# Rotary embedding on one core: two matmul rows of eight in place of three, VectorE sums the other six

## Chip, cores, metric

One core of a Trainium2 chip. The metric is the device time of the core in microseconds (us); the kernel before takes 163.04 us (median of 3 runs, 162.64 to 163.21). A profiled run also has a span, from its first to its last instruction, which here is about 2 us shorter than the device time (161.0 us for 163.02 us).

## The reference

```python
batch, seq, dim = (16, 512, 1024)        # fp32, 16 heads of 64
x = x.reshape(batch, seq, num_heads, head_dim)
x1, x2 = x[..., :half_dim], x[..., half_dim:]
rotated = np.concatenate([x1 * cos - x2 * sin, x1 * sin + x2 * cos], axis=-1)
```

The input is 32 MiB and so is the output; each element takes two products and a sum. cos and sin depend on the sequence position only.

## The kernel before

The data goes through in 8 tiles of 128 partitions x 8 rows x 1024 fp32, 4 MiB each, updated in place in 5 SBUF buffers (in the code NT is the 8 tiles, KK the 8 rows of a tile, P the 128 partitions). For each row two products are summed: `x*cos` (VectorE, into PSUM) and the half-swapped `x*sin`, called `b` (GpSimd, into SBUF). Two ways of summing exist:

- a TensorE row: VectorE writes `x*cos` as two 512-wide halves into single PSUM banks, an identity matmul adds `b` on top of each, ScalarE copies the result back to SBUF;
- a VectorE row: VectorE writes `x*cos` over a two-bank PSUM buffer (`pd`, two of them) and adds `b` itself.

Row 0 is special: VectorE forms its sin product too, in place, so that GpSimd has 7 rows of 8 to do.

```python
PE_ROWS = (0, 3, 6)
DVE_B = ((0,), (0,))
FIRST = (3, 8)
LAST_OUT = (4, 8)            # the last tile is stored in two halves
# ... pools: xp 5 tiles, bp 6 rows, PSUM: pe 3 banks, pd 2 x 2 banks, tables 1 bank
def add(most):
    while len(pending) > most:
        r, ps, b = pending.pop(0)
        nc.vector.tensor_tensor(out=r, in0=ps, in1=b, op=ALU.add)

def finish(t):
    add(0)
    lo = 0
    for hi in LAST_OUT if t == NT - 1 else (KK,):
        store(t, lo, hi)
        lo = hi
    if t + 1 == NT - BUFS:
        for n in range(BUFS, NT):
            load(n)
# ... loads of tiles 0 to 4 are issued at the start, all DMA from one queue (SyncE)
for t in range(NT):
    xt = tiles[t]
    for k in range(KK):
        r = xt[:, k * dim : (k + 1) * dim]
        own = k in DVE_B[t % 2]
        if not own:
            b = bp.tile([P, dim], FP32, name="b")
            # ...
            nc.gpsimd.tensor_tensor(out=halves(b), in0=swapped(r, nh), in1=over_heads(sk), op=ALU.mult)
        if k in PE_ROWS:
            # ... two 512-wide products into ps; for row 0 the sin product in place
            for ps, rc, rhs in parts:
                nc.tensor.matmul(out=ps, lhsT=ident, rhs=rhs, start=False, stop=True, skip_group_check=True)
                nc.scalar.copy(out=rc, in_=ps)
        else:
            add(1)
            ps = pd.tile([P, dim], FP32, name="pd")
            nc.vector.tensor_tensor(out=pairs(ps), in0=pairs(r), in1=cos_b(k, 2 * nh), op=ALU.mult)
            pending.append((r, ps, b))
        if k == 0 and t > 0:
            finish(t - 1)
        add(1)
finish(NT - 1)
```

## Time and profile before

| | before |
|---|---|
| device time, median | 163.04 us |
| span of the profiled run | 161.0 us |
| share of the DMA queue | 97.7% of 16 engines' span |
| VectorE / GpSimd busy | 131.6 / 130.2 us |
| end of VectorE | 142.3 us |
| last store issued, span ends | 142.81 us, 161.0 us |

The page of the kernel before: busy times, then its slices (each digit is the busy share of one of 40 slices, in tenths), then the DMA queue.

```profile
span 161.0 us, 614 instructions
...
PE 76.5 (48%) x103; PEld 24.5 (15%) x103; DVE 131.6 (82%) x142; ACT 29.4 (18%) x49; POOL 130.2 (81%) x62
...
DVE  1059998999999999999999999999999999930000
...
POOL 1039999999999999999999899999999999900000
...
DMA  5999999999999999999999999999999999999993
...
q1 hardware_dynamic: 2752, 67.24, 97.7%
```

VectorE (DVE) and GpSimd (POOL) go to zero in the last tenth of the span, the DMA engines go on.

The groups of VectorE and GpSimd before; after the bars: busy us, mean ns of one, idle time before them.

```profile
L164 POOL TENSOR_TENSOR b<-xt,sns 128x1024 f32<-128x1024 f32 x56 | 129.5, 2349 | 9.8 <-DVE sns L107 9.4
...
L144 DVE TENSOR_TENSOR xt<-pd,b 128x1024 f32<-128x1024 f32 x40 | 48.6, 1218 | 0.0
L182 DVE TENSOR_TENSOR pd<-xt,tab 128x1024 f32<-128x1024 f32 x40 | 48.2, 1223 | 0.3
...
L170 DVE TENSOR_TENSOR ps<-xt,tab 128x512 f32<-128x512 f32 x48 | 30.9, 688 | 0.6 <-ACT xt L178 0.6
```

VectorE in order of time, before (start, length, what). Starts, not lengths, give the cost, since consecutive instructions overlap.

```profile
17.98 1.22 DVE L182 TENSOR_TENSOR pd<-xt,tab 128x1024 f32<-128x1024 f32 x1
19.11 1.22 DVE L144 TENSOR_TENSOR xt<-pd,b 128x1024 f32<-128x1024 f32 x1
20.36 1.23 DVE L182 TENSOR_TENSOR pd<-xt,tab 128x1024 f32<-128x1024 f32 x1
...
139.91 2.35 DVE L144 TENSOR_TENSOR xt<-pd,b 128x1024 f32<-128x1024 f32 x2
```

From product to add there are 1.13 us, from that add to the next product 1.25 us: that product goes into the PSUM buffer which this very add sets free. The last line is where VectorE ends, at 142.26 us.

The SyncE queue before, its last DMA issue, and windows over the end (busy us and count of each engine, then clock, DMA share, GB/s). The columns are PE, PEld, DVE, ACT and POOL. A DMA packet (mostly 1.2 us long here) is counted whole in the window in which it starts, so a share can pass 1.00.

```profile
142.81 0.33 SPq L76 DMA_DIRECT2D out_dram<-xt  x1
```

```profile
138.00:142.00 4.00, 3.58 (x4) 1.17 (x4) 4.00 (x5) 0.59 (x1) 2.63 (x2) 0.50 1.06 459
142.00:150.00 8.00, 0.17 (x1) 0.00 (x0) 0.26 (x1) 0.58 (x1) 0.00 (x0) 0.50 0.94 406
150.00:156.00 6.00, 0.00 (x0) 0.00 (x0) 0.00 (x0) 0.00 (x0) 0.00 (x0) 0.50 1.01 434
```

VectorE ends at 142.26 us and ScalarE's last copy at 142.79 us. From then on no engine computes, and the DMA engines still run at full rate: they work off a backlog.

### The profile page before, as it was taken

To read this page: it belongs to the slowest core of one execution; us is meant where nothing else is said; L and a number is where in the kernel's file an instruction comes from. 1 tells how busy PE (TensorE), PEld (TensorE's weight loads), DVE (VectorE), ACT (ScalarE), POOL (GpSimd) and SP (SyncE) were. 2 spreads that over 40 slices of the span, in tenths; PEclk is the share of its full clock that TensorE was granted. 3 is DMA by queue.
4 is the path that set the end of the run, shared out by engine and by line. 5 is a ranking of instruction groups with operands and counts; after the bars stand their busy time and mean duration, and the time that the engine had idled before them with its cause. 6 is when DMAs were issued, how large, how long until landed. Compare 5 with 4: busy or idle time off the path is not lost.

```text
span 161.0 us, 614 instructions
## 1 busy us (share of the span) xinstructions
PE 76.5 (48%) x103; PEld 24.5 (15%) x103; DVE 131.6 (82%) x142; ACT 29.4 (18%) x49; POOL 130.2 (81%) x62
## 2 busy tenths in 40 slices
PE   3045808534766545618662751765266654630000
PEld 0022102110222012102210211121012210200000
DVE  1059998999999999999999999999999999930000
ACT  0110401402211221221122121212121122010000
POOL 1039999999999999999999899999999999900000
PEclk9999995987655697895579698678955579555555
DMA  5999999999999999999999999999999999999993
GB/s 174 407 412 472 391 488 423 391 464 448 391 440 474 391 415 488 399 415 480 407 415 472 407 415 466 423 415 448 423 423 448 431 423 431 448 415 415 427 436 155
DMA packets 2754, 67.26 MB, mean 418 GB/s; under 512 B 320, under 2 KB 448, under 8 KB 448
## 3 DMA queue, kind: packets, MB, share of 16 engines
q1 hardware_dynamic: 2752, 67.24, 97.7%
q14 instruction: 2, 0.02, 0.0%
HBM read 33.69 MB, written 33.55 MB: 418 GB/s over the span
## 4 chain that ended last, share of the span: by engine, by line
POOL 36%; DMA 22%; DVE 13%; issue 8%; PE 7%; POOLq 1%; ACT 1%; SPq 0%
POOL b L164 36%; DMA xt<-in_x_dram 18%; PE ps L177 6%; DVE xt L144 5%; DMA b<-in_sin_dram 4%; DVE pd L182 4%; DVE ps L170 3%; DVE xt L175 2%; POOLq L218 1%; PE tab L103 1%; ACT xt L178 1%; PE tab L104 1%; DVE sns L106 0%; SPq L72 0%; DVE sns L107 0%
## 5 line engine op out<-in xcount | busy, mean ns | idle before, releaser
L164 POOL TENSOR_TENSOR b<-xt,sns 128x1024 f32<-128x1024 f32 x56 | 129.5, 2349 | 9.8 <-DVE sns L107 9.4
L177 PE MATMUL ps<-b,ident 128*128 128x512 f32 x64 | 48.8, 906 | 43.3 <-POOL b L164 27.5
L144 DVE TENSOR_TENSOR xt<-pd,b 128x1024 f32<-128x1024 f32 x40 | 48.6, 1218 | 0.0
L182 DVE TENSOR_TENSOR pd<-xt,tab 128x1024 f32<-128x1024 f32 x40 | 48.2, 1223 | 0.3
L178 ACT COPY xt<-ps 128x512 f32<-128x512 f32 x48 | 28.1, 585 | 105.9 <-PE ps L177 105.9
L177 PE MATMUL ps<-xt,ident 128*128 128x512 f32 x32 | 24.2, 899 | 16.0 <-issue 6.6
L170 DVE TENSOR_TENSOR ps<-xt,tab 128x512 f32<-128x512 f32 x48 | 30.9, 688 | 0.6 <-ACT xt L178 0.6
L177 PEld LDWEIGHTS ps<-b,ident 128*128 128x128 f32 x64 | 15.2, 263 | 75.3 <-POOL b L164 56.6
L177 PEld LDWEIGHTS ps<-xt,ident 128*128 128x128 f32 x32 | 7.8, 268 | 33.2 <-issue 17.1
L175 DVE TENSOR_TENSOR xt<-xt,tab 128x1024 f32<-128x1024 f32 x8 | 9.8, 1221 | 0.4
L106 DVE TENSOR_SCALAR sns<-tab 128x256 f32<-128x256 f32 x1 | 0.4, 425 | 8.2 <-PE tab L104 8.2
L103 PE MATMUL tab<-b,spread 64*128 64x256 f32 x2 | 1.2, 694 | 5.1 <-DMA b<-in_sin_dram 5.1
L178 ACT ACT_TABLE_LOAD x1 | 1.3, 1283 | 7.5 <-DMA xt<-in_x_dram 7.5
L94 PE MATMUL ps<-zero 128*128 128x512 bf16 x3 | 1.5, 626 | 1.2 <-DVE zero L91 1.2
L103 PEld LDWEIGHTS tab<-b,spread 64*128 64x128 f32 x2 | 0.5, 310 | 6.0 <-issue 6.0
L104 PE MATMUL tab<-b,spread 64*128 64x256 f32 x2 | 1.1, 627 | 0.0
L91 DVE MEMSET zero<- 128x256 uint32 x1 | 0.3, 272 | 0.9 <-PEq L204 0.9
L104 PEld LDWEIGHTS tab<-b,spread 64*128 64x128 f32 x2 | 0.7, 329 | 0.2
L94 PEld LDWEIGHTS <-zero 128*128 128x128 bf16 x3 | 0.3, 125 | 1.5 <-DVE zero L91 1.2
L102 DVE COPY spread<-ident 64x64 f32<-64x64 f32 x2 | 0.3, 182 | 0.2 <-POOL ident masks.py:199 0.2
masks.py:197 POOL MEMSET ident<- 128x128 f32 x1 | 0.2, 204 | 0.3 <-POOLq L204 0.3
L107 DVE COPY sns<-tab 128x256 f32<-128x256 f32 x1 | 0.4, 415 | 0.0
(6 smaller groups left out, 0.9 us busy)
## 6 DMA issues: line engine op xcount, KB each, us to landing
xt<-in_x_dram SPq DMA_DIRECT2D x7, 4096.0 KB, 29.1
out_dram<-xt SPq DMA_DIRECT2D x7, 4096.0 KB, 28.4
out_dram<-xt SPq DMA_DIRECT2D x2, 2048.0 KB, 18.4
xt<-in_x_dram SPq DMA_DIRECT2D x1, 2560.0 KB, 11.5
xt<-in_x_dram SPq DMA_DIRECT2D x1, 1536.0 KB, 6.7
b<-in_sin_dram SPq DMA_DIRECT2D x1, 64.0 KB, 6.5
b<-in_cos_dram SPq DMA_DIRECT2D x1, 64.0 KB, 6.3
```

The lines of the kernel that those rows point to most:

```text
L94: nc.tensor.matmul(out=ps, lhsT=zero[:, :P], rhs=zero, start=True, stop=True)
L103: nc.tensor.matmul(out=sin_t, lhsT=spread, rhs=sin_sb, start=True, stop=True)
L104: nc.tensor.matmul(out=cos_t, lhsT=spread, rhs=cos_sb, start=True, stop=True)
L106: nc.vector.tensor_scalar_mul(out=sns[:, :, 0, :], in0=sin_k, scalar1=-1.0)
L144: nc.vector.tensor_tensor(out=r, in0=ps, in1=b, op=ALU.add)
L164: nc.gpsimd.tensor_tensor(out=halves(b), in0=swapped(r, nh), in1=over_heads(sk), op=ALU.mult)
L170: nc.vector.tensor_tensor(out=pairs(ps), in0=pairs(rc), in1=cos_b(k, BANK // half), op=ALU.mult)
L175: nc.vector.tensor_tensor(out=halves(r), in0=halves(r), in1=swapped_signed(k), op=ALU.mult)
L177: nc.tensor.matmul(out=ps, lhsT=ident, rhs=rhs, start=False, stop=True, skip_group_check=True)
L178: nc.scalar.copy(out=rc, in_=ps)
L182: nc.vector.tensor_tensor(out=pairs(ps), in0=pairs(r), in1=cos_b(k, 2 * nh), op=ALU.mult)
L218: with _tile.TileContext(nc) as tc:
```

## The change

One TensorE row fewer per tile: rows 0 and 4 instead of 0, 3 and 6. VectorE sums six rows instead of five. Relief goes to TensorE (32 matmul calls in the row loop instead of 48; the trace has two records for each, 64 instead of 96) and ScalarE (32 copies instead of 48).

```diff
-PE_ROWS = (0, 3, 6)
+
+PE_ROWS = ((0, 4), (0, 4))
@@
-            if k in PE_ROWS:
+            if k in PE_ROWS[t % 2]:
```

## The prediction

> **What bounds the kernel now.** The DMA engines. The profile's queue table gives the one queue 67.24 MB at a share of 97.7% of 16 engines' span, and the row of slices shows DMA at 9 in every slice but the first and last (418 GB/s over 161.0 us). The Trainium skill ("DMA: Bandwidth & Descriptors", Specifications) states a ceiling of 435 GB/s; this trace agrees, with 437 GB/s from 30 to 50 us. Packet records put the ends of the sixteen 4 MiB transfers (8 loads, 8 stores) 9.7 us apart, from 13.2 to 158.7 us, without a gap.
>
> VectorE (131.6 us, 82%) and GpSimd (130.2 us, 81%) are both full between 10.9 and 142 us, but they finish 17 us before the data does: the last half-tile store is issued at 142.81 us and lands 17 us later, because it stands behind a backlog. The chain of waits blames GpSimd for 36%, but I read compute as having about 10 us of slack against the transfers.
>
> **What the change does, per tile of 8 rows.** A row on TensorE costs VectorE two 128x512 products (688 ns each; 1.19 us of pitch for the pair). A row on VectorE costs a 128x1024 product and a 128x1024 add (1223 and 1218 ns; pitch 1.13 us each, 2.26 us). The Trainium skill ("VectorE: DVE Perf Modes", the fp32 tensor_tensor formula (N+151)/0.96) gives 1224 and 691 ns, which the trace meets. One row per tile moves over: +1.07 us. In the built order, a product that directly follows the add which frees its PSUM buffer occurs three times per tile in place of once; in the trace such a product starts about 0.12 us late (19.11 to 20.36 us). +0.24 us. Together VectorE goes from 16.3 to about 17.55 us a tile, +1.25 to 1.3 us, over 8 tiles about +10 us. GpSimd still needs 16.2 us a tile (7 at a pitch of 2.31 us) and now runs ahead. TensorE loses 32 of 96 fp32 matmuls, ScalarE 16 of 48 copies, both off the path.
>
> **How much lies on the critical path.** I walked the queue with the shifted issue times. Data starts about 1.0 us after an issue on an idle queue (first load: 0.73 to 1.75 us). Loads 5 to 7 still hang on earlier stores' landings (62, 72, 82 us), which don't move. Stores 3 to 5 are issued well before their turn. Store 6: issued about 137.4 us in place of 128.5, queue free at 139.4. First half of tile 7: about 146.6, queue free at 149.1. Last half: VectorE ends at about 152.5 us in place of 142.3, queue free at 153.9. Each is in time, the last two by about 1.5 and 0.3 us. So the slack is nearly all eaten and almost none of the +10 us appears in the time.
>
> **Predicted time:** 163.2 us, range 162.5 to 165.0. Faster by over 2%: 1%; within 2%: 94%; slower by over 2%: 5%.
>
> **What would show each step.** VectorE busy near 140 us, its period per tile near 17.5 us, last VectorE instruction near 152.5 us; TensorE matmul busy down by about a third; GpSimd waiting for free b buffers; last store issued near 152.6 us and landing about 7 us later rather than 17; DMA share still about 97%.
>
> **What would make it wrong.** VectorE waits that I don't see (b not ready, PSUM buffers): every microsecond beyond about 0.5 in the end of VectorE goes straight to the time. A DMA start slower than 1 us late in the run, or uneven engines at the end, would cost 1 to 2 us. Faster would need less traffic.

## The result, and the profile after

The changed kernel takes 162.85 us (median of 6 runs, 162.55 to 163.02) against 163.12 us for the kernel before in the same rounds (6 runs). The ratio is 0.9982, 95% interval 0.9958 to 1.0007: the same. Ratios here and below are the mean time of one kernel's fast runs over that of the other's of the same rounds, so they are not quite the ratio of the medians quoted.

The page of the changed kernel:

```profile
span 160.8 us, 524 instructions
...
PE 62.3 (39%) x71; PEld 20.0 (12%) x71; DVE 141.4 (88%) x142; ACT 20.0 (12%) x33; POOL 130.3 (81%) x62
...
DVE  1059999999999999999999999999999999999800
...
POOL 1039999999999999999999899999999799950000
...
DMA  5999999999999999999999999999999999999994
...
q1 hardware_dynamic: 2752, 67.24, 97.9%
```

The row of VectorE ends about two and a half slices further right; the row of the DMA engines is the same. The groups that changed:

```profile
L183 DVE TENSOR_TENSOR pd<-xt,tab 128x1024 f32<-128x1024 f32 x48 | 58.1, 1225 | 0.8
L145 DVE TENSOR_TENSOR xt<-pd,b 128x1024 f32<-128x1024 f32 x48 | 58.4, 1218 | 0.0
...
L171 DVE TENSOR_TENSOR ps<-xt,tab 128x512 f32<-128x512 f32 x32 | 20.6, 688 | 0.0
```

Eight products and eight adds more, sixteen half products fewer, and no duration has changed. VectorE in order of time:

```profile
15.63 1.22 DVE L145 TENSOR_TENSOR xt<-pd,b 128x1024 f32<-128x1024 f32 x1
16.88 1.23 DVE L183 TENSOR_TENSOR pd<-xt,tab 128x1024 f32<-128x1024 f32 x1
18.02 1.22 DVE L145 TENSOR_TENSOR xt<-pd,b 128x1024 f32<-128x1024 f32 x1
19.15 1.28 DVE L171 TENSOR_TENSOR ps<-xt,tab 128x512 f32<-128x512 f32 x2
...
149.72 2.35 DVE L145 TENSOR_TENSOR xt<-pd,b 128x1024 f32<-128x1024 f32 x2
```

The late start (15.63 to 16.88 us, 1.25 us) now comes three times a tile. VectorE ends at 152.07 us, 9.8 us later than before. The last two stores (the halves of the last tile), and windows over the end:

```profile
146.22 0.33 SPq L77 DMA_DIRECT2D out_dram<-xt  x1
152.14 0.33 SPq L77 DMA_DIRECT2D out_dram<-xt  x1
```

```profile
138.00:142.00 4.00, 1.63 (x2) 0.05 (x1) 3.97 (x5) 1.13 (x2) 3.77 (x2) 0.76 1.05 451
142.00:150.00 8.00, 3.58 (x4) 1.17 (x4) 7.93 (x9) 1.17 (x2) 0.73 (x1) 0.79 0.95 408
150.00:156.00 6.00, 0.00 (x0) 0.00 (x0) 2.06 (x2) 0.00 (x0) 0.00 (x0) 0.51 1.00 429
```

The DMA columns are those of before (0.95 and 0.94, 1.00 and 1.01), while VectorE is now busy to 152 us. The last store is issued 9.3 us later and yet lands at nearly the same moment (159.69 us, before 159.92 us): from issue to landing it takes 7.6 us in place of 17.1 us, as there is less queue before it.

### The profile page after: what moved, and what is told of

It reads as the page before. It is cut to its first block, busy times and chain, and to the rows that moved or that the text cites. A ratio compares the mean times of both kernels' runs of the same rounds, so it can differ in the third digit from the quotient of the medians.

```text
span 160.8 us, 524 instructions
## 1 busy us (share of the span) xinstructions
PE 62.3 (39%) x71; PEld 20.0 (12%) x71; DVE 141.4 (88%) x142; ACT 20.0 (12%) x33; POOL 130.3 (81%) x62
## 3 DMA queue, kind: packets, MB, share of 16 engines
q1 hardware_dynamic: 2752, 67.24, 97.9%
## 5 line engine op out<-in xcount | busy, mean ns | idle before, releaser
L183 DVE TENSOR_TENSOR pd<-xt,tab 128x1024 f32<-128x1024 f32 x48 | 58.1, 1225 | 0.8
L145 DVE TENSOR_TENSOR xt<-pd,b 128x1024 f32<-128x1024 f32 x48 | 58.4, 1218 | 0.0
L178 PE MATMUL ps<-xt,ident 128*128 128x512 f32 x32 | 29.5, 1077 | 48.6 <-issue 38.1
L178 PE MATMUL ps<-b,ident 128*128 128x512 f32 x32 | 29.4, 1073 | 29.8 <-DVE ps L171 27.1
L179 ACT COPY xt<-ps 128x512 f32<-128x512 f32 x32 | 18.7, 585 | 120.3 <-PE ps L178 120.3
L171 DVE TENSOR_TENSOR ps<-xt,tab 128x512 f32<-128x512 f32 x32 | 20.6, 688 | 0.0
L178 PEld LDWEIGHTS ps<-xt,ident 128*128 128x128 f32 x32 | 9.4, 324 | 68.2 <-issue 63.6
L178 PEld LDWEIGHTS ps<-b,ident 128*128 128x128 f32 x32 | 9.2, 316 | 49.7 <-issue 25.6
```

Source lines behind the costliest of these rows:

```text
L171: nc.vector.tensor_tensor(out=pairs(ps), in0=pairs(rc), in1=cos_b(k, BANK // half), op=ALU.mult)
```

## The experiments

Two theories:

- **Transfers.** The 16 DMA engines bind both kernels. Compute had some 10 us of slack before the change and has almost none after it. What VectorE gained in work came out of that slack.
- **Compensation (the rival).** VectorE and GpSimd, both full, bind the kernel. The 10 us on VectorE are paid back by the relief of TensorE, ScalarE and GpSimd, so that moving a row is neutral as such.

The experiments come in three groups: take traffic away, take compute away or add to it, and spoil the end of the queue. Kernels are compared only within the same rounds.

### Half of every store left out (e1, e2)

The same edit in both kernels; the results are wrong.

```diff
         for hi in LAST_OUT if t == NT - 1 else (KK,):
-            store(t, lo, hi)
             lo = hi
+        store(t, KK // 2, KK)
```

> The kernel before, but each tile stores only its rows 4 to 7, issued when the tile is finished (results wrong on purpose). Transfer theory (the 16 DMA engines bind, compute has about 10 us of slack in the kernel before and almost none in the changed one): with a quarter of the traffic gone the compute binds; VectorE still ends near 142.3 us, the last store is issued near 142.8 us onto an idle queue and the span ends 7.9 us later, near 150.7 us; time about 152.6 us, 0.936 of before. Rival theory (compute binds, and what the change adds to VectorE is paid back by relief of TensorE, ScalarE and GpSimd): time near 163 us less a shorter tail, and, above all, the same as its twin made from the changed kernel.

> The changed kernel with the same half stores (results wrong on purpose). Transfer theory: VectorE ends near 152.1 us, last store issued near 152.15 us, span near 160.0 us, time about 161.9 us: 6% slower than its twin made from the kernel before, and only about 1 us faster than the changed kernel itself, which is the slack it has left. Rival theory: within 1% of its twin.

Measured: 151.6 us from the kernel before (ratio to before 0.9293) and 161.09 us from the changed one (0.9872). One over the other is 1.062: with a quarter of the traffic gone, the change costs 9.5 us. Windows over the end of e2 (first line 138 to 142 us):

```profile
138.00:142.00 4.00, 1.33 (x2) 0.00 (x0) 3.97 (x4) 0.83 (x2) 3.77 (x2) 0.83 1.08 459
142.00:150.00 8.00, 3.45 (x4) 1.18 (x4) 7.93 (x9) 1.17 (x2) 0.43 (x1) 0.76 0.00 0
150.00:156.00 6.00, 0.00 (x0) 0.00 (x0) 1.75 (x2) 0.00 (x0) 0.00 (x0) 0.50 0.62 262
```

By the packet records all 16 DMA engines stand still from 142.59 to 152.65 us: they wait for VectorE. So the cost of the change is real and of the predicted size; in the full kernels it is hidden. That contradicts the rival, which expected the twins within 1%. The expectation was 0.8 to 1 us too long for both: on an idle queue the last half tile ends the span 7.3 us after its issue (142.58 to 149.9 and 151.82 to 159.1 us), not 7.9 us; in the packet records its data starts 0.83 us after the issue, not 1.0. The rest is that VectorE ended 0.3 us earlier than expected in both (142.02 and 151.76 us).

### Transfers alone (e3)

```diff
-    for t in range(NT):
-        xt = tiles[t]
-        for k in range(KK):
-            ...                       # the whole row loop
+    for t in range(NT - 1):
+        finish(t)
     finish(NT - 1)
```

> The kernel before without its row loop: every tile is loaded and stored again as it is (results wrong on purpose), same issues in the same order. Transfer theory: the time stays within 1% of before, about 162.5 us, with DMA busy about 97% of the span and 9.7 us for each 4 MiB. Rival theory: well below, by more than 5%, as the transfers alone would not fill the span.

Measured: 162.47 us, ratio 0.9958 (0.9932 to 0.9985). The queue of this run, from its page:

```profile
DMA  6999999999999999999999999999999999999994
...
q1 hardware_dynamic: 2752, 67.24, 97.9%
```

Loading and storing the data untouched takes almost as long as the kernel. All the compute of the kernel before adds about 0.6 us to that. The run also bears out the Trainium skill ("SBUF — State Buffer", Who interferes with whom), which says that DMA does not contend with compute engines: in the packet records 4 MiB take 9.7 us in this run, with the engines empty, as in the kernel before, with VectorE and GpSimd full.

### Four TensorE rows (e8)

```diff
-PE_ROWS = ((0, 4), (0, 4))
+PE_ROWS = ((0, 2, 4, 6), (0, 2, 4, 6))
```

> Four rows of eight on TensorE (0, 2, 4, 6), VectorE sums the other four. Transfer theory: time within 1% of before, about 163 us. VectorE needs only about 15.1 us a tile, GpSimd with 16.2 us a tile now paces it, VectorE waits some 9 us for b, and VectorE still ends near 141 to 142 us. Rival theory (VectorE's own work binds the kernel before): faster than before by several us.

Measured: correct, 163.29 us, ratio 1.0005 (0.998 to 1.0029). VectorE's work falls to 123.0 us busy and nothing is gained. But VectorE's end hardly moves either (142.13 us, before 142.26 us), as GpSimd's seven rows a tile now pace it. So this run tells against VectorE's own work as the bound, not against GpSimd's; against GpSimd speak e3, and e4 with e5 below. Of VectorE's groups, the two that now wait:

```profile
L171 DVE TENSOR_TENSOR ps<-xt,tab 128x512 f32<-128x512 f32 x64 | 41.9, 689 | 7.1 <-ACT xt L179 5.6 <-DMA xt<-in_x_dram 1.5
...
L145 DVE TENSOR_TENSOR xt<-pd,b 128x1024 f32<-128x1024 f32 x32 | 38.9, 1215 | 2.0 <-POOL b L165 2.0
```

The 9.1 us of waiting were expected, their place was not quite: 5.6 us are waits for ScalarE to empty a PSUM half, 1.5 us a wait for a load, and only 2.0 us are direct waits for `b`. That ScalarE is late because the matmul before it waits for GpSimd is likely (TensorE waits 35.5 us for `b` in all), but was not tested apart.

### The last tile stored in one piece (e4, e5)

The same edit in both kernels. The first half of the last tile can then leave only when the whole tile is done.

```diff
-LAST_OUT = (4, 8)
+LAST_OUT = (8,)
```

> The kernel before with the last tile stored in one piece, issued when all its rows are done (near 142.8 us). Transfer theory: the queue is busy with earlier stores until 149.1 us, so nothing changes: about 163.0 us, ratio 1.00. Rival theory (the end of compute sets the end): about 4.9 us slower, as half the tile can no longer go out early.

> The changed kernel with the same one-piece last store, issued near 152.1 us. Transfer theory: the queue runs dry from 149.1 to about 153.2 us, one DMA gap of about 4 us, span near 164.9 us, time about 166.8 us, 1.023 of before. The same edit that is free in the kernel before costs 4 us here. Rival theory: the same effect in both kernels.

Measured: 163.08 us in the kernel before (ratio 0.9997, 0.9975 to 1.0019) and 165.86 us in the changed one (1.0167, 1.0145 to 1.0189). The same edit is free where there is backlog and costs about 3 us where there is none (the second lies within 2%, but its interval is clear of 1). Windows over the end, e4:

```profile
145.00:149.00 4.00, 0.00 (x0) 0.00 (x0) 0.00 (x0) 0.00 (x0) 0.00 (x0) 0.50 1.14 492
149.00:153.00 4.00, 0.00 (x0) 0.00 (x0) 0.00 (x0) 0.00 (x0) 0.00 (x0) 0.50 0.95 410
```

and e5:

```profile
145.00:149.00 4.00, 1.85 (x3) 0.34 (x1) 3.93 (x4) 1.17 (x2) 0.00 (x0) 0.80 0.91 393
149.00:153.00 4.00, 0.00 (x0) 0.00 (x0) 2.81 (x3) 0.00 (x0) 0.00 (x0) 0.63 0.30 131
```

The store is issued at 151.88 us in e5, and the queue runs dry before it. By the packet records all 16 engines are idle for 3.2 us (149.54 to 152.71 us); 4 us had been expected. In e4 it is issued at 142.43 us, well before its turn. The rival expected the same effect in both.

### More rows for VectorE (e6, e7)

One more row moved in every other tile (e6), and in every tile (e7).

```diff
-PE_ROWS = ((0, 4), (0, 4))
+PE_ROWS = ((0, 4), (0,))      # e6
+PE_ROWS = ((0,), (0,))        # e7
```

> The changed kernel with one more row moved to VectorE in each odd tile (row 0 alone on TensorE there). Four rows more at about 1.3 us each: VectorE ends near 157.3 us. Transfer theory: the slack is gone, so the end of VectorE goes one for one into the time: span = end of VectorE + about 7.9 us = 165.2 us, time about 167.0 us, 1.025 of before. Rival theory (moving rows costs nothing, as in the change itself): 163 us.

> One row of eight on TensorE in every tile (row 0). Eight rows more than the changed kernel at about 1.3 us each: VectorE ends near 162.6 us. Transfer theory: span near 170.5 us, time about 172.3 us, 1.057 of before, so about 9.5 us above the changed kernel where the change itself, of the same size, cost nothing. Rival theory: 163 us.

Measured, both correct: 166.6 us (ratio 1.0212, 1.0185 to 1.0238) and 171.65 us (1.0524, 1.0504 to 1.0544). VectorE ends at 157.5 and 162.4 us (157.3 and 162.6 expected). From e6 to e7 four rows cost 5.05 us. Windows over the end of e7:

```profile
140.00:145.00 5.00, 0.07 (x1) 0.10 (x1) 4.91 (x6) 0.00 (x0) 4.70 (x2) 0.50 0.02 7
145.00:149.00 4.00, 3.68 (x4) 1.08 (x4) 4.00 (x4) 0.87 (x2) 2.35 (x1) 0.52 0.62 262
```

VectorE is full throughout, while by the packet records no packet is under way from 142.30 to 146.85 us (the 0.02 of the first window leaves out packets that started before 140 us): the roles are exchanged. Put in one table, with the moment of the last store's issue from the queue's timeline and the end of the span:

| TensorE rows of the 64 | kernel | last store issued | span | from issue to end |
|---|---|---|---|---|
| 32 | e8 | 142.72 | 161.53 | 18.8 |
| 24 | before | 142.81 | 161.00 | 18.2 |
| 16 | after | 152.14 | 160.77 | 8.6 |
| 12 | e6 | 157.54 | 164.91 | 7.4 |
| 8 | e7 | 162.46 | 169.82 | 7.4 |

On an idle queue a half tile needs 7.3 us (e1, e2). What a kernel has over that is its slack: 10.9 us before, 1.3 us after, next to nothing in e6 and e7. The change moved the last issue by 9.3 us, and the slack fell by 9.6 us. One step further, the same kind of edit costs almost its full size.

### The late start of a product (e9, e10, e11)

Of the 9.8 us, some 2 us were put down to a product that starts 0.12 us late when the add just before it frees its PSUM buffer. To test it, half a product of row 4 is moved in between at one of three such places in each tile. The arithmetic stays the same, the waits are in place; only the order on VectorE changes.

```diff
             else:
                 add(1)
+                if k == 3:
+                    early.append(half_product(4, xt[:, 4 * dim : 5 * dim], 0))
                 ps = pd.tile([P, dim], FP32, name="pd")
```

(and row 4 then takes its first half from `early`). e10 is the same with the half stores of e1 and e2, wrong; e11 is the changed kernel itself again.

> The changed kernel, correct, with row 4's first half product moved between the add of row 1 and the product of row 3, which needs the PSUM buffer that this add frees. If such a product starts 0.12 us late because it waits for the add just before it, one of three such waits per tile goes: VectorE's last instruction ends about 1.0 us (8 x 0.12) before 152.1 us, near 151.1 us. If the 0.12 us has another cause (the switch of operands, say), it ends at 152.1 us as before. The time stays with the transfers in both cases: within 0.5% of before.

> The same reordering with the half stores (results wrong on purpose), where compute binds. Transfer theory: what VectorE saves now shows in the time: about 1.0 us below the 161.1 us of its twin without the reordering, near 160.1 us, ratio to before about 0.982; if the waits are not removed, 161.1 us (0.987).

> The changed kernel unaltered, on the same chip as the two others: 162.9 us, 0.998 of before, VectorE's end near 152.1 us and last store issued near 152.1 us.

Measured: e9 is correct and takes 162.58 us (ratio 0.9978, 0.9943 to 1.0014); e10 takes 159.88 us (0.981, 0.9781 to 0.9839); e11 takes 162.54 us (0.9971, 0.9942 to 1.0). VectorE in e9:

```profile
15.36 1.22 DVE L145 TENSOR_TENSOR xt<-pd,b 128x1024 f32<-128x1024 f32 x1
16.50 0.69 DVE L162 TENSOR_TENSOR ps<-xt,tab 128x512 f32<-128x512 f32 x1
17.09 1.22 DVE L190 TENSOR_TENSOR pd<-xt,tab 128x1024 f32<-128x1024 f32 x1
...
21.08 1.22 DVE L145 TENSOR_TENSOR xt<-pd,b 128x1024 f32<-128x1024 f32 x1
22.33 1.23 DVE L190 TENSOR_TENSOR pd<-xt,tab 128x1024 f32<-128x1024 f32 x1
```

At the edited place the add is followed after 1.14 us and the half product after 0.59 us; at a place left alone (21.08 to 22.33 us) the 1.25 us remain. VectorE ends at 150.77 us in e9 and at 151.70 us in e11. Its first product starts at 10.63 and 10.55 us, so from there to the end it is 1.0 us shorter, the 8 x 0.12 us expected. The other cause named, the switch of operands, does not fit: the half product too follows the add directly and writes PSUM, and it is not late. So the term was rightly read. In the time it shows where compute binds (e10 against e2: 0.981 against 0.987, about 1 us) and not where the transfers bind (e9 against e11).

No correct version here is clearly faster than the kernel before: e3, with no compute at all, is at 162.47 us, so with these transfers in this order there is at most about 0.4% to be had.

## Why the prediction was right

**The bound.** It named the DMA engines. e3 shows it: the transfers alone take 162.47 us. The chain in the page of the kernel before puts 36% of the span on GpSimd; e3 shows that this was not the bound. e8 adds that less work for VectorE gains nothing.

**The cost of the change.** Predicted +1.25 to 1.3 us a tile and an end of VectorE at about 152.5 us; measured 152.07 us. Later tiles are 1.31 us longer: their first products start 17.6 us apart on average (27.39 to 133.18 us over six tiles) in place of 16.3 us. Eight times that is 10.5 us; the kernel before also had one wait of 0.6 us for ScalarE in its second tile, which is gone. The 0.12 us in it are shown by e9.

**Where it went.** Predicted: into the slack. e1 and e2 uncover it (9.5 us), e4 and e5 show that the backlog at the end of the queue is what it consisted of, and e6 and e7 show what happens when it is used up.

**How much slack is left.** Predicted were margins of about 1.5 us for the first half of the last tile and 0.3 us for the last half, "nearly all eaten". In the same measure they are about 1.9 and 0.9 us: by the packet records the queue reaches the two halves at 149.0 and 153.9 us in the mean of the 16 engines, as predicted (149.1 and 153.9), and on an idle queue their data would start at 147.05 and 152.97 us (issue plus 0.83 us). The table, which counts at the end of the span, has 1.3 us for the last half. Two terms were mis-sized, both on the safe side: the end of VectorE (0.4 us too late) and the start of data after an issue (1.0 us assumed from the first load; 0.83 us in e1, e2, e5 and e7). The tail of a last half tile on an idle queue had likewise been put at 7.9 us and is 7.3; besides the start, it holds 1.4 us from the last data to the end of the span (148.49 to 149.9 us in e1, 157.74 to 159.1 us in e2). So the expected times of e1, e2, e5, e6 and e7 came out 0.4 to 1 us too long.

**Signs in the profile.** VectorE busy 141.4 us (140), DMA share 97.9% (97%), last store issued at 152.14 us (152.6) and landing 7.6 us later (about 7): as predicted. GpSimd's waits were barely to be seen (1.9 us, until VectorE's adds had freed buffers): it did run ahead and ended near 143 us. One sign was wrong: TensorE's matmul busy time was to fall by a third, and fell from 76.5 to 62.3 us. The number of matmul records fell by a third (96 to 64 in the row loop), but each became longer (mean 906 or 899 ns before, 1073 or 1077 after), while the mean granted clock fell from 0.746 to 0.659. The mean clock alone does not explain it: e9 and e10 give TensorE the same work and ran at mean clocks of 0.606 and 0.816, with records of 1085 and 986 ns in the one and 1076 and 1001 ns in the other. The cause stays open. VectorE waited for TensorE and ScalarE only 0.6 us before and not at all after, so it did not matter.

**Open.** The changed kernel came out a shade below the kernel before in both comparisons (0.9982 and 0.9971, intervals reaching 1). Whether there is a true 0.2% cannot be told from these runs.

## What to carry to other kernels

When several engines are at nine tenths, look at the right edge of their rows: the time from the last store's issue to the end of the span, less what that store needs on an idle queue, is the slack of everything else. (Look for earlier gaps too: in e6 and e7 the queue already ran dry for 0.9 and 4.6 us before the last whole tile's store.) Compute can be added up to that slack for nothing and costs its full price beyond it, so a "free" change may leave the kernel at the edge, where the next harmless edit (e5) does cost. To weigh such a change, measure it with part of the transfers taken away, where its cost can be seen.

## What the Trainium skill lacked or had wrong

- "DMA: Bandwidth & Descriptors", Where 436 GB/s comes from: it says that for transfers between HBM and SBUF the HBM side, about 358 GB/s, binds. For this program on one core that is too low: it moved 67 MB at 418 GB/s over its whole span, 437 GB/s from 30 to 50 us, near the page's other ceiling, 435 GB/s. The page itself has 425 GB/s for one core in its table of measurements; only the flat sentence is wrong. Which part of the path sets the rate was not tested here.
- "VectorE: DVE Perf Modes", The DRAIN you can't avoid: it reports that a semaphore after each of 8 copies costs nothing extra, and leaves out the case where an instruction waits for the one directly before it. Here a VectorE product that waits for the VectorE add directly before it starts 1.25 us after that add, against 1.13 us without such a wait; another instruction between them takes the 0.12 us away (e9).
- "DMA: Bandwidth & Descriptors", Specifications: its 0.6 us to the first byte does not say from where it counts. Here data starts 0.83 us after the start of the issuing instruction (0.33 us long), on an idle queue in e1, e2, e5 and e7, and 1.02 us after it for the first load of the kernel before (0.73 to 1.75 us).
